# Channel sums on VectorE, weights' low parts by adding DMAs, and block-diagonal values with the mean as a bias, in a two-block sequence model on one core

## The chip, the cores and the metric

One core of a Trainium2 chip runs the whole program: two layers of a first block and one layer of a second block, on 512 positions of 1024 channels. The metric is device time in microseconds.

## The reference

All arithmetic is float32. A layer of the first block mixes by two branches, then adds a cross-attention and a gated feed-forward part; the second block follows. The change touches the mixing part only:

```python
def mlstm_branch(xm, z, ...):
    xc = silu(causal_dwconv(xm, conv_w, conv_b))
    q, k, v = blockdiag(xc, wq), blockdiag(xc, wk), blockdiag(xm, wv)   # blocks of 4x4
    gates = concatenate([q, k, v]) @ w_gate + b_gate
    h = mlstm_chunkwise(heads(q), heads(k), heads(v), i_pre, f_pre)     # 4 heads of 256
    hn = (h - mean(h)) * rsqrt(var(h) + 1e-5)
    return ((hn * norm_g + skip * xc) * silu(z)) @ w_down

def conformer_conv_branch(a, g, ...):
    u = causal_dwconv(a * sigmoid(g), dw_w, dw_b)                       # 31 taps
    u = silu(layernorm(u, ln_g, ln_b))                                  # mean and variance over 1024 channels
    return u @ w_pw + b_pw
```

## The kernel before

Channels lie on partitions (8 tiles of 128), the 512 positions on columns. Every float32 product is made of three in a faster format: `wsplit` loads a weight block of 128x1024 (512 KB) into `r`, ACT rounds it into a high part `h`, and VectorE takes `l = r - h`. `dense` runs 8 x 3 matmuls of 128x512 per output tile: high weights by high and low operand, low weights by high operand. The buffers of `h` and `l` turn over in threes (`wh`), those of `r` in twos. All loads are issued from SyncE's queue (line 183); GpSimd (POOL) has no DMA.

`mix` is the part in question, once per layer. It projects the conformer's gate and value (16 dense products), then multiplies small block-diagonal weights with each other (float32 matmuls of 36 and 128 columns), then runs the 8 mLSTM projections with their convolution of 4 taps, then the gates, then 4 heads. 16 more dense products, the output gates, are set among the gates' chain and the heads as fillers (`fill`). Then come 8 products for `z` with the mLSTM's output `ym`, then the products by `ml_w_down`, then those by `cv_w_pw`.

The conformer's convolution of 31 taps (`conv31`) is background work on VectorE: 248 steps, handed out a few per dense product (`pump`) at a low priority, into 8 tiles `acc`. The layer norm over channels needs two sums over all 1024 channels. Before, `totals` multiplies each of the 8 tiles by a matrix of ones in plain float32 and lets PSUM add them; first the tiles, then their squares once the mean is subtracted.

The values of a head come from `xm` by block-diagonal weights from which the mean over the head is taken: ACT adds a bias to the weights, which makes 256 columns per half head full, so each position block needs two float32 matmuls of 256 columns added together.

The order on each engine is made at build time by a scheduler that plays the program on a timeline; rows of that order stand with the change below. Names in the trace are cut: `h` and `l` are the weights' parts, `r` the raw block, `p` a PSUM tile, `t` and `w` other tiles.

Of the kernel before, what the change touches and what calls it, by code (L numbers as in the profile page):

```python
# [20 lines left out]
P = 128  # L21
# [8 lines left out]
# columns of the parameter arrays (per layer: mixers, the rest; second block): name -> (first column, columns)  # L30
# [29 lines left out]
def consts():  # L60
    """Identity; where a chunk's key is in reach; 2^100 where the time lies behind."""
    s, t = np.arange(P)[:, None], np.arange(P)[None, :]
    c = np.stack([s == t, (s <= t) & (s // 64 == t // 64), s > t]).astype(np.float32)
    c[2] = np.where(s > t, np.float32(2.0**100), np.float32(0))
    return c


def consts2():
    """Row selectors [36, 4, 128] (rows h and 32 + h) and the scan's resets."""
    c = np.zeros((2, P, T), np.float32)  # L70
    for h in range(4):
        c[0, [h, 32 + h], P * h : P * h + P] = 1.0
    c[1] = (np.arange(T) % 64 != 0).astype(np.float32)[None, :]
    return c
# [13 lines left out]

class Net:
    def __init__(self, tc, D, es):  # L90
# [11 lines left out]
        self.bg, self.rate, self.debt = [], 0.0, 0.0  # L102
        self.ahead = []
# [81 lines left out]
    def pump(self):  # L185
        """Some of the background work."""
# [14 lines left out]
    def split_into(self, h, l, src, scale=None):  # L201
        """The two parts of src * scale, a high one of 12 bits and the rest."""
# [17 lines left out]
    def wsplit(self, src, k, n):  # L220
        """A weight block [128, k, n] from DRAM and its two parts."""
# [4 lines left out]
        self.split_into(h, l, r)  # L226
        return h, l

    def dense(self, W, m, ops, n=T, mw=P):
        """PSUM [mw, n] = W[:, tile m]^T @ ops (list of (hi, lo) per 128 channels)."""  # L230
# [12 lines left out]
    def rsqrt(self, v, eps, y):  # L243
        """y = -2 / sqrt(v + eps); v in PSUM or SBUF."""
# [22 lines left out]
    def totals(self, xs, which):  # L267
        """total of several tiles"""
        ps = self.psum(tag="pf")
        for j, x in enumerate(xs):  # L270
            self.mm(ps, self.ones[:, which], x, j == 0, j == len(xs) - 1)
        return ps

    def square(self, x):
        q = self.w()
        self.act(q, x, AF.Square)
        return q

    def parts(self, xs, g, tag="hn"):
        """The parts of x * g (g a column per tile)."""  # L280
        return [self.split(x, g[:, j : j + 1], tag=tag) for j, x in enumerate(xs)]

    def norm(self, xs, g, tag="hn"):
        """rms norm; g holds the gain times -1/2. The parts of x * g, and what their products are to be times."""
# [44 lines left out]
    def silu2(self, pre):  # L329
        """2 * silu(pre), in place."""  # L330
# [16 lines left out]
    def gate(self, d, W, m, j, ops, bias=0.0):  # L347
        """tanh of half a gate, kept in DRAM."""
# [5 lines left out]
    def gated(self, d, j, ps):  # L354
        """(1 + the kept tanh) * ps"""
# [4 lines left out]
    def rows_bcast(self, src):  # L360
        """[4, T] float32 as the parts of one operand [36, T]; read with self.sel."""
# [6 lines left out]
    def conv31(self, u, acc):  # L368
        """Background steps: depthwise conv of u (twice its value)."""
        for j in range(KT):  # L370
# [8 lines left out]

            self.bg.append(first)  # L380
            for k in range(29, -1, -1):
                self.bg.append(lambda k=k, j=j: tap(k, j))

    def mix(self, l, xs, xd):
# [4 lines left out]
        u, acc = [], []  # L389
# [20 lines left out]
        # products of the weights: gates from xc and xm, scores from xc alone  # L410
# [26 lines left out]
        # the values' weights less their means over the heads  # L437
# [4 lines left out]
        wv = []  # L442
        for h in range(4):
            b = self.t((P, 2, 256))
            self.dma(b, D["wv"][l][:, 2 * h : 2 * h + 2])
            for c in range(2):
                self.act(b[:, c], b[:, c], AF.Identity, bias=r[:, 2 * h + c : 2 * h + c + 1])
            wv.append(b)
        # mLSTM: conv and gate (xc twice its value)
        xm, xc = [], []  # L450
        xcd = self.dp.tile([KT, P, T], F32, name=self.nm("xcd"))
        for j in range(KT):
            if j == BV:
# [3 lines left out]
                self.act(ev, pe, AF.Copy)  # L457
            pm = self.dense(win, j, hn)
# [21 lines left out]
        # gates  # L480
# [4 lines left out]
        bi, bf = self.pc("gate_b", 0)[:4], self.pc("gate_b", 1)[32:36]  # L485
        W4 = (4, T)
        f, i_, B = self.t(W4), self.t(W4), self.t(W4)
        self.act(f, pg[32:36], AF.Identity, bias=bf)
        self.act(i_, pg[0:4], AF.Identity, bias=bi)
# [17 lines left out]
        pu = self.psum((P, 4, 4), tag="pf")  # L507
        for j in range(4):
            nc.tensor.transpose(pu[:, j], i_[:, P * j : P * j + P], self.ident[:4, :4])
        uT = self.small((P, 4, 4), 2, "uT")  # L510
# [4 lines left out]
        for h in range(4):  # L515
# [14 lines left out]
            for k0 in (0, 2):  # L530
                pv = self.psum((P, 2, 256))
                for k in (k0, k0 + 1):
                    for c in range(2):
                        self.mm(pv[:, k - k0], xm[2 * h + c][:, P * k : P * k + P], wv[h][:, c], c == 0, c == 1)
                a, b = self.split(pv, shape=(P, 2, 256))
# [41 lines left out]
        fill(16)  # L577
        y, vv = self.w(W4), self.w(W4)
# [28 lines left out]
        # conformer branch: layer norm, swish  # L607
        pmu = self.totals(acc, 0)
        mg = []
        for j in range(KT):  # L610
# [4 lines left out]
            if j == 1:  # L615
                for k in range(KT):
                    self.tt(acc[k], acc[k], pmu, ALU.subtract)
                r = self.rsqrt(self.totals([self.square(c) for c in acc], 0), 1, self.t(tag="R"))
# [32 lines left out]
    def memory(self):  # L651
        """The parts of the normalised memory."""
# [137 lines left out]
    def between(self, xs):  # L790
        """The first block's norm and at once the second block's first one."""
# [34 lines left out]
    def finish(self, w2, a, xs, out):  # L826
        """The last tile of the sum, the norm and the stores, one half of the times after the other."""
# [20 lines left out]
    def cmul(self, ore, oim, are, aim, bre, bim, tmp, neg=False):  # L848
        """(are + i aim)(bre + i bim); with neg, the negated imaginary part."""
# [582 lines left out]
```

## Time and profile before

| | us |
|---|---|
| median of 3 runs (lowest, highest) | 3160.26 (3159.73, 3161.98) |
| profiled execution, span | 3160.4 |
| TensorE busy | 3120.6 (99%) |
| weight loads busy (beside matmuls) | 2548.6 (81%) |
| VectorE busy | 2098.6 (66%) |
| ScalarE busy | 1351.1 (43%) |
| GpSimd busy | 0.7 (0%) |
| DMA, mean share of 16 engines | 35.2% |

The span runs from the first to the last instruction of the profiled execution, which is one more run; it stands as that execution's own time. A busy time counts time in which at least one instruction of the engine ran. A float32 matmul shows as two records, one in the faster format as one.

### The profile page before, as it was taken

The page shows a single profiled execution, that of the slowest core. Times are in us where ns is not written, and L with a number is a line of the kernel's source. Part 1 is how long each engine was busy: PE and PEld are TensorE (multiplying, and loading weights), DVE is VectorE, ACT ScalarE, POOL GpSimd, SP SyncE. Part 2 cuts the span into 40 slices and gives each one's busy share as a digit, 9 for nine tenths or more (in the row PEclk, how much of TensorE's full clock was granted, in tenths as well). Part 3 has the DMA queues.
Part 4 walks back from the last instruction along what each step waited for, and adds up shares of the span by engine and source line. Part 5 has one row for each costly group of instructions (what it writes and reads, how often), then busy time and mean ns, then how long its engine had stood idle before and what let it go on. Part 6 is the DMA issues. An engine that isn't in the chain of part 4 may idle for free. (4 is left out here: it accounts for less than half of the span.)

```text
span 3160.4 us, 37385 instructions
## 1 busy us (share of the span) xinstructions
PE 3120.6 (99%) x14508; PEld 2548.6 (81%) x14508; DVE 2098.6 (66%) x3191; ACT 1351.1 (43%) x1923; POOL 0.7 (0%) x5
## 2 busy tenths in 40 slices
PE   8989999999999999999999999999999999999998
PEld 7867778888888887777888888888888788788887
DVE  8988975558773798886556876365534873655533
ACT  6444454446552444445444555332223433442222
POOL 0000000000000000000000000000000000000000
PEclk9999999999999999999999999999999999999999
DMA  5322443323333433245332333332333354532332
GB/s 174 118 89 80 163 148 122 114 80 100 96 103 114 121 117 106 76 161 161 112 107 87 100 97 94 96 100 95 99 102 116 107 142 120 190 100 94 100 94 87
DMA packets 135041, 354.29 MB, mean 112 GB/s; under 512 B 23472, under 2 KB 31936, under 8 KB 134864
## 3 DMA queue, kind: packets, MB, share of 16 engines
q1 hardware_dynamic: 134864, 351.92, 35.2%
q8 instruction: 113, 1.85, 0.2%
q14 instruction: 64, 0.52, 0.1%
HBM read 318.60 MB, written 29.85 MB: 110 GB/s over the span
## 5 line engine op out<-in xcount | busy, mean ns | idle before, releaser
L180 PE MATMUL p<-t,h 128*128 128x512 f32 (+1 forms) x8092 | 2470.7, 387 | 12.8 <-ACT h L167 10.7
L180 PEld LDWEIGHTS p<-t,h 128*128 128x128 f32 x8092 | 1507.0, 188 | 335.5 <-issue 16.5
L180 PE MATMUL p<-t,l 128*128 128x512 f32 (+1 forms) x4046 | 1561.4, 387 | 3.6 <-DVE l L170 2.6
L167 ACT ACTIVATE h<-r 128x1024 fp32r<-128x1024 f32 (+2 forms) x541 | 556.7, 1030 | 1301.6 <-PE p L180 826.5
L170 DVE TENSOR_TENSOR l<-r,h 128x1024 fp32r<-128x1024 f32 (+2 forms) x541 | 640.4, 1185 | 435.4 <-ACT h L167 434.3
L180 PEld LDWEIGHTS p<-t,l 128*128 128x128 f32 x4046 | 761.3, 188 | 164.3 <-DVE l L170 5.7
L177 DVE SCALAR_TENSOR_TENSOR t<-t,mph,t 128x489 f32<-128x489 f32 (+19 forms) x480 | 341.4, 729 | 6.8 <-ACT t L167 2.3
L180 PE MATMUL p<-t,t 128*128 128x256 f32 (+9 forms) x1528 | 258.5, 319 | 2.8 <-DVE t L170 2.0
L170 DVE TENSOR_TENSOR w<-p,t 128x512 f32<-128x512 f32 (+1 forms) x204 | 124.0, 622 | 191.7 <-PE p L180 189.4
L180 PEld LDWEIGHTS p<-t,t 128*128 128x128 f32 (+5 forms) x1528 | 199.1, 178 | 51.4 <-issue 18.3
L167 ACT ACTIVATE t<-w 128x512 fp32r<-128x512 f32 (+2 forms) x204 | 121.2, 598 | 165.6 <-DVE w L170 100.4
L170 DVE TENSOR_TENSOR t<-p,t 128x512 fp32r<-128x512 f32 (+2 forms) x156 | 96.9, 632 | 125.1 <-PE p L180 94.8
L177 DVE SCALAR_TENSOR_TENSOR t<-w,t 128x512 fp32r<-128x512 f32 (+1 forms) x208 | 141.9, 685 | 16.8 <-ACT t L167 14.8
L177 DVE SCALAR_TENSOR_TENSOR w<-w,fp,w 128x511 f32<-128x511 f32 (+1 forms) x176 | 131.8, 749 | 13.4 <-ACT w L167 10.3
L167 ACT ACTIVATE w<-w,fp 128x512 f32<-128x512 f32 x176 | 134.5, 764 | 8.7 <-DVE w L170 5.6
L167 ACT ACTIVATE w<-t 128x512 f32<-128x512 f32 (+2 forms) x160 | 95.1, 609 | 31.1 <-DVE t L177 15.4
L170 DVE TENSOR_TENSOR w<-w,w 128x512 f32<-128x512 f32 (+2 forms) x153 | 102.3, 674 | 8.3 <-ACT w L167 6.6
L167 ACT ACTIVATE w<-w 128x512 f32<-128x512 f32 (+2 forms) x110 | 68.0, 620 | 69.9 <-DVE w L177 66.5
L177 DVE SCALAR_TENSOR_TENSOR w<-w,w 128x512 f32<-128x512 f32 (+2 forms) x115 | 78.2, 681 | 27.9 <-ACT w L167 27.8
L167 ACT ACTIVATE t<-p 128x512 fp32r<-128x512 f32 (+3 forms) x118 | 61.8, 537 | 73.2 <-PE p L180 56.2
L170 DVE TENSOR_TENSOR w<-p,w 128x512 f32<-128x512 f32 x45 | 31.0, 691 | 74.2 <-PE p L180 74.2
L180 PE MATMUL p<-h,t 128*128 128x256 f32 (+1 forms) x320 | 68.5, 306 | 0.0
(147 smaller groups left out, 1213.6 us busy)
## 6 DMA issues: line engine op xcount, KB each, us to landing
r<-ffn_w SPq DMA_DIRECT2D x120, 512.0 KB, 3.4
r<-w_in SPq DMA_DIRECT2D x96, 512.0 KB, 3.5
r<-ffn_w_up SPq DMA_DIRECT2D x88, 512.0 KB, 3.5
r<-ffn_w_down SPq DMA_DIRECT2D x32, 512.0 KB, 3.6
r<-w_out SPq DMA_DIRECT2D x24, 512.0 KB, 3.6
tg<-g SPq DMA_DIRECT2D x32, 256.0 KB, 2.0
r<-ml_w_down SPq DMA_DIRECT2D x16, 512.0 KB, 3.5
w<-tg SPq DMA_DIRECT2D x32, 256.0 KB, 4.4
```

The costliest lines, as they stand in the source:

```text
L167: self.nc.scalar.activation(out, in_, f, **k)
L170: self.nc.vector.tensor_tensor(out=out, in0=a, in1=b, op=op)
L177: self.nc.vector.scalar_tensor_tensor(out=out, in0=a, scalar=s, in1=b, op0=op0, op1=op1)
L180: self.nc.tensor.matmul(ps, lhsT=l, rhs=r, start=start, stop=stop)
```

## The change

Three edits, all in `mix` and what it calls:

- Sums: `conv31` also adds the finished tiles into one tile on VectorE, as background; the squares are added on VectorE by `sumsq`. One matmul by ones each (`total`) replaces eight.
- Low parts: from before the mLSTM projections to the last head (`lean`), `wsplit` writes `-h` into `l` by a second ACT copy, and a DMA from GpSimd's queue adds the weights from DRAM to it. That holds for 8 projections and 16 output gates per layer.
- Values: the weights stay block-diagonal (two matmuls of 128 columns in place of two added ones of 256). The negated mean of the weights goes as four more columns into the gates' product, comes out as four more rows, is transposed with the gates, and is added to the values as a bias when these are split.

```diff
+class Tiles(list):
+    sum = None
...
         self.dma(r, src)
-        self.split_into(h, l, r)
+        if not self.lean:
+            self.split_into(h, l, r)
+            return h, l
+        self.act(h, r, AF.Copy)
+        self.act(l, r, AF.Copy, scale=-1.0)
+        self.nc.gpsimd.dma_start(out=l, in_=src, accum_op=ALU.add)
         return h, l
...
-    def totals(self, xs, which):
-        ps = self.psum(tag="pf")
-        for j, x in enumerate(xs):
-            self.mm(ps, self.ones[:, which], x, j == 0, j == len(xs) - 1)
-        return ps
...
+            def add(j=j):
+                if j == 1:
+                    acc.sum = self.t(tag="R")
+                if j:
+                    self.tt(acc.sum, acc[0] if j == 1 else acc.sum, acc[j], ALU.add)
...
-        for h in range(4):
-            b = self.t((P, 2, 256))
-            self.dma(b, D["wv"][l][:, 2 * h : 2 * h + 2])
-            for c in range(2):
-                self.act(b[:, c], b[:, c], AF.Identity, bias=r[:, 2 * h + c : 2 * h + c + 1])
-            wv.append(b)
+        wv = blocks("wv")
+        self.lean = True
...
+                for h in range(4):
+                    nc.vector.tensor_copy(out=ev[:, 2 * h : 2 * h + 2, 4 + h], in_=r[:, 2 * h : 2 * h + 2])
...
-            nc.tensor.transpose(pu[:, j], i_[:, P * j : P * j + P], self.ident[:4, :4])
+            nc.tensor.transpose(pu[:, j], i8[:, P * j : P * j + P], self.ident[:8, :8])
...
-                        self.mm(pv[:, k - k0], xm[2 * h + c][:, P * k : P * k + P], wv[h][:, c], c == 0, c == 1)
-                a, b = self.split(pv, shape=(P, 2, 256))
+                        self.mm(pv[:, k - k0, P * c : P * c + P], xm[2 * h + c][:, P * k : P * k + P], wv[2 * h + c])
+                a, b = (self.t((P, 2, 256), F32R) for _ in range(2))
+                for k in range(2):
+                    mean = uT[:, k0 + k, 4 + h : 5 + h]
+                    self.act(a[:, k], pv[:, k], AF.Identity, bias=mean)
+                    self.stt(b[:, k], pv[:, k], mean, a[:, k].bitcast(F32), ALU.add, ALU.subtract)
...
         fill(16)
+        self.lean = False
...
-        pmu = self.totals(acc, 0)
+        pmu = self.total(acc.sum, 0)
...
-                r = self.rsqrt(self.totals([self.square(c) for c in acc], 0), 1, self.t(tag="R"))
+                r = self.rsqrt(self.total(self.sumsq(acc), 0), 1, self.t(tag="R"))
```

The order of the instructions moves with it. First place: TensorE in layer 0, from the last product of the gates (p_1487) to the transposes (by `identr`) and the broadcasts (by `sel`). p_1712, p_1630, p_1673 and p_1716 are dense products of the output gates. Before:

```order
L180 MATMUL p_1487<-t_1481,t_995 36x512
L180 MATMUL p_1487<-t_1471,t_993 36x512
L180 MATMUL p_1712<-t_319,h_1714 128x512
...
L180 MATMUL p_1712<-t_355,l_1715 128x512
L180 MATMUL p_1764<-t_1092,t_1003 128x512
...
L180 MATMUL p_1772<-t_1146,t_1004 128x512
L509 MATMUL p_1755<-identr,t_1521 128x4 x4
L180 MATMUL p_1780<-t_1539,sel 128x512
```

and with the change:

```order
L187 MATMUL p_1487<-t_1481,t_995 36x512
L187 MATMUL p_1487<-t_1471,t_993 36x512
L187 MATMUL p_1630<-t_331,l_1633 128x512
...
L187 MATMUL p_1630<-t_355,l_1633 128x512
L187 MATMUL p_1673<-t_313,h_1675 128x512
...
L187 MATMUL p_1716<-t_355,l_1719 128x512
L514 MATMUL p_1759<-identr,t_1521 128x8 x4
L187 MATMUL p_1776<-t_1136,t_1004 128x512
L187 MATMUL p_1786<-t_1539,sel 128x512
```

Between the last gate product and the transposes stood 27 matmuls; now 66 do.

Second place: VectorE at the end of the conformer's convolution in layer 0. The tap of 128x482 is the last; p_3132 and p_3172 hold the mean; l_ is a low part of the next weights. Before:

```order
L177 SCALAR_TENSOR_TENSOR t_3143<-w_3141,p_3144 128x512
L177 SCALAR_TENSOR_TENSOR t_1744<-t_918,mph_91,t_1744 128x482
L177 SCALAR_TENSOR_TENSOR t_3178<-w_3176,p_3179 128x512
L170 TENSOR_TENSOR l_3363<-r_3361,h_3362 128x1024
L170 TENSOR_TENSOR l_3398<-r_3396,h_3397 128x1024
L170 TENSOR_TENSOR t_461<-t_461,p_3132 128x512
```

and with the change:

```order
L184 SCALAR_TENSOR_TENSOR t_1853<-t_918,mph_91,t_1853 128x482
...
L177 TENSOR_TENSOR t_734<-t_734,t_1853 128x512
...
L177 TENSOR_TENSOR t_461<-t_461,p_3172 128x512
...
L177 TENSOR_TENSOR t_1853<-t_1853,p_3172 128x512
L177 TENSOR_TENSOR w_3254<-w_3252,w_3254 128x512
L184 SCALAR_TENSOR_TENSOR t_3176<-w_3174,p_3177 128x512
L184 SCALAR_TENSOR_TENSOR t_3211<-w_3209,p_3212 128x512
L177 TENSOR_TENSOR l_3396<-r_3394,h_3395 128x1024
L177 TENSOR_TENSOR l_3431<-r_3429,h_3430 128x1024
```

The two low parts stood ahead of the eight subtractions of the mean and now stand behind them.

Third place: ACT in the mLSTM projections of layer 0. Before:

```order
L167 ACTIVATE h_1588<-r_1587 128x1024
L167 ACTIVATE t_1417<-p_1378,mp_90 128x512
L167 ACTIVATE t_1200<-t_1192 128x512
L167 ACTIVATE t_1419<-t_1417,mp_90 128x512
L167 ACTIVATE w_1261<-t_1256 128x512
L167 ACTIVATE h_1630<-r_1629 128x1024
```

and with the change:

```order
L174 ACTIVATE h_1588<-r_1587 128x1024
L174 ACTIVATE t_1416<-p_1376,mp_90 128x512
L174 ACTIVATE l_1589<-r_1587 128x1024
L174 ACTIVATE t_1418<-t_1416,mp_90 128x512
L174 ACTIVATE t_1260<-t_1252 128x512
L174 ACTIVATE w_1312<-t_1307 128x512
L174 ACTIVATE h_1632<-r_1631 128x1024
```

The second copy of the block stands behind the evacuation of a projection.

## Rows read from the trace of the kernel before

**Rows 1.** The page's first part: span, and busy time of TensorE.

```profile
span 3160.4 us, 37385 instructions
PE 3120.6 (99%) x14508; PEld 2548.6 (81%) x14508; DVE 2098.6 (66%) x3191; ACT 1351.1 (43%) x1923; POOL 0.7 (0%) x5
```

**Rows 2.** Waits of TensorE: who, for whom, us in total, times, longest.

```profile
PE p L180 <- DVE t L170: 8.0, 4, 4.9
PE p L509 <- DVE t L170: 3.8, 1, 3.8
```

**Rows 3.** Stretches: length, then busy time by engine, granted clock, DMA share, GB/s.

```profile
104.00:160.00 56.00, 56.00 (x252) 44.94 (x252) 54.53 (x82) 29.31 (x45) 0.00 (x0) 0.97 0.39 132
160.00:330.00 170.00, 161.32 (x732) 122.40 (x731) 145.69 (x217) 73.12 (x130) 0.00 (x0) 0.97 0.27 89
```

**Rows 4.** Timeline of TensorE, channel sums: start, us, instruction, count.

```profile
383.97 6.17 PE L180 MATMUL p<-t,ones 128*128 128x512 f32 x14
...
1408.83 7.03 PE L180 MATMUL p<-t,ones 128*128 128x512 f32 x16
```

**Rows 5.** The page's groups: additions of 128x512 on VectorE.

```profile
L170 DVE TENSOR_TENSOR w<-w,w 128x512 f32<-128x512 f32 (+2 forms) x153 | 102.3, 674 | 8.3 <-ACT w L167 6.6
```

**Rows 6.** Timeline of TensorE, values of a head in layers 0 and 1.

```profile
264.74 1.89 PE L180 MATMUL p<-t,t 128*128 128x256 f32 x8
...
1232.62 3.62 PE L180 MATMUL p<-t,t 128*128 128x256 f32 x16
```

**Rows 7.** Timeline of TensorE, float32 matmuls of few columns in layer 1.

```profile
1137.21 5.52 PE L180 MATMUL p<-t,t 128*128 128x36 f32 x48
...
1158.91 1.87 PE L180 MATMUL p<-t,t 128*128 128x36 f32 x16
```

**Rows 8.** Timeline of TensorE, the gates of layer 0; idle before in brackets.

```profile
188.37 1.61 PE L180 MATMUL p<-t,t 128*36 128x512 f32 x4
...
194.79 1.52 PE L180 MATMUL p<-t,t 128*128 128x512 f32 x6
200.08 0.55 PE L509 MATMUL p<-identr,t 4*128 4x4 f32 x4 [3.76 <-DVE t L170]
205.55 1.22 PE L180 MATMUL p<-t,sel 36*128 36x512 f32 x2 [4.92 <-DVE t L170]
...
211.75 0.81 PE L180 MATMUL p<-t,h 128*128 128x512 f32 x2
```

**Rows 9.** Stretches around that hole, columns as in rows 3.

```profile
206.00:208.00 2.00, 2.00 (x5) 1.16 (x5) 1.97 (x4) 1.05 (x3) 0.00 (x0) 0.50 0.00 0
...
210.00:212.00 2.00, 2.00 (x11) 1.77 (x10) 1.93 (x4) 0.60 (x1) 0.00 (x0) 1.00 0.00 0
```

**Rows 10.** Timelines of ACT and VectorE in the mLSTM projections of layer 0.

```profile
141.91 1.06 ACT L167 ACTIVATE h<-r 128x1024 fp32r<-128x1024 f32 x1 [1.91 <-PE p L180]
...
147.35 1.06 ACT L167 ACTIVATE h<-r 128x1024 fp32r<-128x1024 f32 x1 [2.95 <-PE p L180]
148.32 0.67 ACT L167 ACTIVATE t<-p,mp 128x512 f32<-128x512 f32 x1
...
149.25 1.22 DVE L170 TENSOR_TENSOR l<-r,h 128x1024 fp32r<-128x1024 f32 x1
```

**Rows 11.** DMA: the queue; then issues with count, KB each, median us to landing.

```profile
q1 hardware_dynamic: 134864, 351.92, 35.2%
...
r<-w_in SPq DMA_DIRECT2D x96, 512.0 KB, 3.5
...
t<-wkT SPq DMA_DIRECT2D x4, 256.0 KB, 6.6
```

**Rows 12.** Timelines of TensorE and VectorE at the channel mean of layer 0.

```profile
399.74 1.13 PE L180 MATMUL p<-t,ones 128*128 128x512 f32 x2 [0.51 <-DVE t L177]
...
402.61 0.50 PE L180 MATMUL p<-t,l 128*128 128x512 f32 x1 [1.28 <-DVE l L170]
...
402.47 4.86 DVE L170 TENSOR_TENSOR t<-t,p 128x512 f32<-128x512 f32 x8
```

More of the change, by code (lines that the diff above doesn't have):

```diff
@@ L265, in total @@
         return ps
-    def totals(self, xs, which):
-        ps = self.psum(tag="pf")
-        for j, x in enumerate(xs):
-            self.mm(ps, self.ones[:, which], x, j == 0, j == len(xs) - 1)
-        return ps
[L274 to L277, printed above, removed]
     def parts(self, xs, g, tag="hn"):
@@ L382, in conv31 @@
                 self.bg.append(lambda k=k, j=j: tap(k, j))
+            self.bg.append(add)
     def mix(self, l, xs, xd):
@@ L388, in mix @@
         raw, R = self.norm(xs, g, "hd")
-        u, acc = [], []
+        u, acc = [], Tiles()
         for j in range(KT):
@@ L441, in mix @@
         self.ts(r, r, -1.0 / 256, ALU.mult)
-        wv = []
-        for h in range(4):
-            b = self.t((P, 2, 256))
-            self.dma(b, D["wv"][l][:, 2 * h : 2 * h + 2])
-            for c in range(2):
-                self.act(b[:, c], b[:, c], AF.Identity, bias=r[:, 2 * h + c : 2 * h + c + 1])
-            wv.append(b)
+        wv = blocks("wv")
+        self.lean = True
         xm, xc = [], []
@@ L484, in mix @@
             self.mm(pg, ev[:, j], xm[j], False, j == KT - 1)
-        bi, bf = self.pc("gate_b", 0)[:4], self.pc("gate_b", 1)[32:36]
+        bi, bf = self.pc("gate_b", 0)[:8], self.pc("gate_b", 1)[32:36]
         W4 = (4, T)
-        f, i_, B = self.t(W4), self.t(W4), self.t(W4)
+        f, i8, B = self.t(W4), self.t((8, T)), self.t(W4)
+        i_ = i8[0:4]
         self.act(f, pg[32:36], AF.Identity, bias=bf)
-        self.act(i_, pg[0:4], AF.Identity, bias=bi)
+        self.act(i8, pg[0:8], AF.Identity, bias=bi)
         e = self.w(W4)
@@ L506, in mix @@
         fill(FILLS[0])
-        pu = self.psum((P, 4, 4), tag="pf")
+        pu = self.psum((P, 4, 8), tag="pf")
         for j in range(4):
-            nc.tensor.transpose(pu[:, j], i_[:, P * j : P * j + P], self.ident[:4, :4])
-        uT = self.small((P, 4, 4), 2, "uT")
+            nc.tensor.transpose(pu[:, j], i8[:, P * j : P * j + P], self.ident[:8, :8])
+        uT = self.small((P, 4, 8), 2, "uT")
         self.act(uT, pu, AF.Copy)
@@ L577, in mix @@
         fill(16)
+        self.lean = False
         y, vv = self.w(W4), self.w(W4)
@@ L1380, in layout @@
         o[n] = both(lambda l: blockdiag(A[s][l]).transpose(2, 1, 0))
-    b = np.zeros((DEPTH, P, 4, 2, 2, P), np.float32)
-    v = both(lambda l: blockdiag(A["ml_wv"][l])).reshape(DEPTH, P, 4, 2, P)
-    for c in range(2):
-        b[:, :, :, c, c] = v[:, :, :, c]
-    o["wv"] = b.reshape(DEPTH, P, KT, 256)
+    o["wv"] = both(lambda l: blockdiag(A["ml_wv"][l]))
     o["wvn"] = A["ml_wv"].reshape(DEPTH, KT, P, 4).transpose(0, 2, 1, 3)
```

## The prediction

> **What bounds the kernel now.** I read the page's first part, then TensorE's waits, then a table of stretches. TensorE is busy 3120.6 of 3160.4 us [rows 1], so about 40 us of the span are not its work, and nearly every matmul taken out shortens the kernel. The waits show the largest of those 40 us: one of 3.76 us before a transpose (L509) and one of 4.92 us behind VectorE [rows 2]. Both lie in layer 0, near 200 us. The stretches show why: in the first layer's mLSTM projections (104 to 160 us) VectorE is busy 54.53 of 56.00 us, and TensorE all of them; in the gates and heads (160 to 330 us) TensorE loses 8.7 us while VectorE works 145.69 of 170 us [rows 3]. VectorE is the second bound, in that part only. Layer 1 runs the same code without such waits. The profiled execution (span 3160.4 us) lies 0.1 us from the median of the three runs, 3160.26, so the sum is made against 3160.4.
>
> **A. Channel sums.** The change removes 14 float32 matmuls of 128x512 per layer (two totals of eight become two of one), 28 in all. A float32 matmul has two records. Sixteen of them in a row take 7.03 us and fourteen 6.17 us [rows 4], so two records, one matmul, are 0.86 us. 28 x 0.86 = **24.1 us** off TensorE. In return VectorE gets 14 additions of 128x512 per layer at 0.67 us [rows 5], 9.4 us. Seven run as background among the convolution taps, and the subtractions taken off VectorE (D) more than pay for those. The seven that add the squares stand on the path, see E.
>
> **B. Values.** Per layer 32 float32 matmuls lose half their columns (256 to 128). Sixteen records of the long form take 3.62 us and eight 1.89 us: 1.73 us for four matmuls, 0.43 us each [rows 6]. For the short form, a row of 48 records takes 5.52 us; by the code 32 of them have 36 columns, the other 16 have 128. Sixteen of 36 columns alone take 1.87 us, 0.117 each, so the 16 of 128 columns take 5.52 - 32 x 0.117 = 1.78 us, 0.22 us per matmul [rows 7]. 64 x (0.43 - 0.22) = **13.4 us**. The bias makes two ACT and two VectorE instructions out of one each, and eight activations on weights go; both engines have idle time there [rows 3], so nothing on the path.
>
> **C. The hole in layer 0.** The chain of gates (sigmoid, two scans, the broadcast of the maximum) keeps the transposes waiting until 200.08 and the broadcasts until 205.55; TensorE had run dry at 196.3 [rows 8]. Its granted clock fell to 0.50 after it went idle, that is from the 2.4 to the 1.2 GHz level, and was back by 210 [rows 9]; the work from 205.55 to 211.75 would take 0.23 x 3 + 8 x 0.43 = 4.1 us at the level before, so 2 us more are lost. The hole is 3.76 + 4.92 + 2.0 = 10.7 us. The order of TensorE shows what fills it: before, 27 matmuls stand between the last gate product and the transposes, now 66. At 5.44 us per 24 [rows 10] that is 6.1 us of cover before and 15.0 us now, against a chain of about 15.6 us from the last gate product (190.0) to the broadcasts. I take **10 us**.
>
> **D. Adding DMAs.** For 24 weight blocks per layer, 48 in all, VectorE's subtraction (1.22 us) becomes an ACT copy as long as the first (1.06 us) [rows 10] and a DMA from POOL's queue that adds 512 KB. POOL had no work in this part, so nothing queues behind it there. ACT gets 25 us per layer and has 27 of 56 and 97 of 170 us free [rows 3]. VectorE loses 29 us per layer. TensorE must not wait for a low part. Dense products follow one another every 5.44 us; three buffers turn over. From a released buffer: 1.06 + 0.67 (the evacuation that now stands between) + 1.06 = 2.8 us on ACT, the DMA, then 5.0 us from the first use of the low part to the product's end. Three buffers carry that without loss while (2.8 + D + 5.0)/3 is at most 5.44, so D up to **8.5 us** is free. No row shows an adding DMA. Bounds: a plain load of the block lands in 3.5 us; the slowest loads in a crowd land 256 KB in 6.6 us [rows 11], so twice that, 13.2 us, is the other end. I take twice the plain load, 7 us, since it reads two operands where a load reads one and its row is the nearest: **0 us**. At the lower end nothing is gained either, as TensorE doesn't wait on low parts there now. At 13.2 us each product takes 7.0 instead of 5.44; 8 projections and about 5 gates per layer stand back to back, so 26 x 1.56 = 41 us are lost.
> The Trainium skill (Collectives: The Full Stack, "The bandwidth ceiling") has the DMA engines add at half the rate of a copy because two sources are read; no run here shows it.
>
> **E. New waits.** Taking work from TensorE takes cover away. Layer 0: the order of VectorE now has the last tap, the last sum, and then all eight subtractions of the mean before the low parts of the next weights; before, those low parts stood first and TensorE waited 0.51 + 1.28 us [rows 12]. Eight subtractions take 4.86 us [rows 12]. From the mean's matmul I count 1.9 us to the first three, 0.6 for the last low part of the mLSTM output, 3.1 for five more, 1.8 for three short operations and 2.3 for two low parts: 10 us, in which TensorE has about 4.5 us of work. That is 5 us idle; 3 more where the eight-fold sum used to fill time while VectorE finished the outputs. Layer 1: between the mean and the total of squares stand 33 matmuls (7.5 us), while the chain between them is 4.9 us of subtractions, 7 x 0.67 of additions, and 4 us of other VectorE work between them: 13.6 us, so 6 us idle. Less the 1.8 us that go, 12 us; with 2 us for a fallen clock as in C, **+14 us**. Bounds: 0 (VectorE, with 29 us less to do, runs ahead) and 24.1 (all of A given back).
>
> **Sum:** 24.1 + 13.4 + 10 - 14 = 33.5 us, so 3160.4 - 33.5 = **3127 us**.
>
> **Rivals.**
> 1. *No new waits.* E is nothing: 3160.4 - 47.5 = 3113 us. For it: layer 1 has no wait on VectorE now. Against: the order of VectorE puts long work ahead of what TensorE needs. Chance 0.20.
> 2. *VectorE's chain takes back the sums.* E is all of A (24.1 us: 3137 us), up to A and B together (37.5 us: 3150 us). For it: VectorE is the last to finish in layer 0 [rows 12]. Chance 0.12.
> 3. *The DMA engines become the bound; slower.* A load's work per engine: 0.352 x 16 x 3160.4 us for 351.92 MB [rows 11] is 1.66 us per 512 KB. With an adding DMA of k loads, a product costs (1 + k) x 1.66 us of every engine. Up to k = 2.3 this stays under 5.44. It eats the whole gain when a product takes 33.5/26 = 1.29 us more, at k = 3.1 (5.1 us per adding DMA); at k = 4 it takes 8.3 us, 26 x 2.86 = 74 us, so 3201 us. For it: the share of the DMA engines is already 0.39 in that stretch [rows 3]. Against: two reads and a write are not four loads. Chance 0.13.
> 4. *POOL can't issue beside VectorE; slower.* VectorE works without a gap for tens of us in this stretch. If an issue must wait for one, and 10 us come on top of the 7, D is 17 us, a product takes 8.3 us, and the time is again 3201 us. No row has POOL at work beside VectorE. The Trainium skill (SBUF — State Buffer, the "DVE blocks DMA" trap) states that such a DMA's descriptors are written by GpSimd, which VectorE can lock out of a shared port; its section "Who interferes with whom" narrows that for two-input instructions, which nearly all here are, to GpSimd work that reads SBUF. By that rule this is unlikely. Chance 0.05.
>
> That the change doesn't do what it says is no rival: the order shows the removed matmuls gone and 48 adding DMAs on POOL's queue.
>
> **How the numbers follow.** My forecast has 0.50, the rivals 0.20, 0.12, 0.13 and 0.05. A measurement tells about 0.2% from no change, 6.3 us. The forecast, rival 1 and rival 2 are faster by more, but for 0.02 of slack on the last: 0.80. That and the mild end of rival 3 (0.03) fall within: 0.05. Slower is the rest of rivals 3 and 4: 0.15. The range runs from 3108 us (rival 1 and 5 us of waits elsewhere that a freer VectorE removes) to 3172 us (D at its upper bound, 3127 + 41, and a little); it leaves out the worst of rivals 3 and 4 and little below.
>
> **What would show it.** Right: TensorE's busy time down by some 38 us; no wait near 200 us in layer 0 and no fall of the clock there; waits of about 5 us on VectorE in each layer around the total of the squares; low parts landing within 8.5 us. Wrong: TensorE waiting for a DMA of low parts during the projections, a DMA share near 1 there, or products more than 5.44 us apart.

## The result, and the profile after

The changed kernel took 3128.71 us (median of 4 runs, 3125.27 to 3130.98); the kernel before, on the same chip, 3159.99 (4 runs, 3156.57 to 3161.98). The ratio is **0.9899, 95% interval 0.9886 to 0.9912**: about 32 us faster. The forecast was 3127.0 us, range 3108 to 3172. The profiled execution of the changed kernel took 3125.27 us with a span of 3123.5, so it lies 3.4 us below its median.

The page of the changed kernel: span, busy times, the DMA queues (packets, MB, share of 16 engines), and the loads and adding DMAs of weights (`w_in` holds those of the projections; KB each, median us to landing).

```profile
span 3123.5 us, 37404 instructions
...
PE 3085.6 (99%) x14452; PEld 2528.4 (81%) x14452; DVE 2068.9 (66%) x3195; ACT 1391.9 (45%) x1971; POOL 42.2 (1%) x53
...
q1 hardware_dynamic: 134288, 350.87, 36.4%
q0 software_dynamic: 6912, 25.17, 4.3%
...
r<-w_in SPq DMA_DIRECT2D x96, 512.0 KB, 4.0
...
l<-w_in POOLq DMA_DIRECT2D x48, 512.0 KB, 6.9
...
r<-ml_w_down SPq DMA_DIRECT2D x16, 512.0 KB, 3.6
```

TensorE is busy 35.0 us less than in [rows 1]. A second queue is there, and an adding DMA lands in 6.9 us.

Stretches of the changed kernel, columns as in [rows 3].

```profile
104.00:160.00 56.00, 56.00 (x249) 42.41 (x248) 55.14 (x93) 36.75 (x51) 6.91 (x8) 1.00 0.88 209
160.00:330.00 170.00, 170.00 (x808) 130.89 (x808) 145.92 (x229) 95.10 (x161) 11.22 (x13) 1.00 0.57 147
...
360.00:380.00 20.00, 15.79 (x66) 11.76 (x64) 18.38 (x33) 10.54 (x17) 0.00 (x0) 1.00 0.25 87
380.00:400.00 20.00, 17.66 (x65) 14.04 (x66) 13.71 (x19) 9.52 (x12) 0.00 (x0) 0.83 0.31 107
1340.00:1400.00 60.00, 54.62 (x221) 41.56 (x220) 48.15 (x71) 28.21 (x41) 0.00 (x0) 0.97 0.45 156
1380.00:1400.00 20.00, 14.62 (x50) 9.66 (x49) 16.83 (x25) 10.25 (x14) 0.00 (x0) 0.91 0.17 53
```

From 160 to 330 us TensorE works without a gap; before it lost 8.7 us there [rows 3]. The DMA share in the projections rose from 0.39 to 0.88, and TensorE lost nothing by it. The idle time sits elsewhere now: 4.2 and 2.3 us from 360 to 400 in layer 0, and 5.4 us from 1380 to 1400 in layer 1, with the granted clock at 0.83 and 0.91 as means of the stretches. Those two places are where each layer takes the channel mean and the total of squares.

TensorE's timeline in the changed kernel: the transposes and broadcasts of the gates, then the two places.

```profile
193.56 0.41 PE L514 MATMUL p<-identr,t 8*128 8x8 f32 x4
...
194.33 0.49 PE L187 MATMUL p<-t,sel 36*128 36x512 f32 x1
...
371.69 1.02 PE L187 MATMUL p<-t,ones 128*128 128x512 f32 x2
...
375.29 0.50 PE L187 MATMUL p<-t,h 128*128 128x512 f32 x1 [1.89 <-DVE t L184]
...
378.39 0.73 PE L187 MATMUL p<-t,h 128*128 128x512 f32 x2 [1.45 <-ACT h L174]
382.35 0.80 PE L187 MATMUL p<-t,l 128*128 128x512 f32 x1 [3.22 <-DVE l L177]
382.94 1.05 PE L187 MATMUL p<-t,h 128*128 128x512 f32 x2
...
387.96 0.61 PE L187 MATMUL p<-t,h 128*128 128x512 f32 x2
...
1388.69 0.96 PE L187 MATMUL p<-t,h 128*128 128x512 f32 x3 [2.47 <-ACT t L174]
...
1392.62 0.74 PE L187 MATMUL p<-t,h 128*128 128x512 f32 x2 [0.93 <-ACT h L174]
1394.96 2.08 PE L187 MATMUL p<-w,ones 128*128 128x512 f32 x2 [1.61 <-DVE w L177]
```

The hole of 3.76 and 4.92 us at the gates [rows 8] is gone: transposes and broadcasts have no idle time before them. In layer 0 three waits, 6.6 us in all, follow the mean; in layer 1 four, 5.4 us. VectorE's timeline in layer 0 shows what stands ahead of the operands that TensorE waits for.

```profile
368.97 0.72 DVE L184 SCALAR_TENSOR_TENSOR t<-t,mph,t 128x482 f32<-128x482 f32 x1
...
372.75 1.88 DVE L177 TENSOR_TENSOR t<-t,p 128x512 f32<-128x512 f32 x3 [1.18 <-PE p L187]
374.55 0.68 DVE L184 SCALAR_TENSOR_TENSOR t<-w,t 128x512 fp32r<-128x512 f32 x1
375.15 3.07 DVE L177 TENSOR_TENSOR t<-t,p 128x512 f32<-128x512 f32 x5
378.13 0.69 DVE L177 TENSOR_TENSOR w<-w,w 128x512 f32<-128x512 f32 x1
...
379.93 2.36 DVE L177 TENSOR_TENSOR l<-r,h 128x1024 fp32r<-128x1024 f32 x2
```

The sum by ones is one matmul now, 1.02 us at 371.69, where fourteen records took 6.17 [rows 4] and two more 1.13 [rows 12]. VectorE: last tap at 368.97, three subtractions of the mean, the last low part of the mLSTM's output (374.55, TensorE's wait of 1.89), five subtractions, the first addition of squares; only behind them two low parts of weights (379.93), for which TensorE waits 3.22 us. On ACT, squares stand ahead of the high parts of the next weights as well (three from 373.53, one at 376.78). But the first of these high parts, at 375.82, waits 0.47 us for TensorE, so the squares are not the whole of the wait of 1.45 us.

In layer 1 TensorE waits for no low part of weights. VectorE has done the eight subtractions by 1386.8; only then comes the product that ends the mLSTM's last output, and ACT's copy of it, for which TensorE waits 2.47 us:

```profile
1387.28 0.69 DVE L177 TENSOR_TENSOR w<-w,t 128x512 f32<-128x512 f32 x1
...
1388.01 0.63 ACT L174 ACTIVATE t<-w 128x512 fp32r<-128x512 f32 x1
```

### The profile page after: what moved, and what is told of

Same layout as the page of the kernel before. It is cut to its first block, busy times and chain, and to the rows that moved or that the text cites. A ratio compares the mean times of both kernels' runs of the same rounds, so it can differ in the third digit from the quotient of the medians.

```text
span 3123.5 us, 37404 instructions
## 1 busy us (share of the span) xinstructions
PE 3085.6 (99%) x14452; PEld 2528.4 (81%) x14452; DVE 2068.9 (66%) x3195; ACT 1391.9 (45%) x1971; POOL 42.2 (1%) x53
## 3 DMA queue, kind: packets, MB, share of 16 engines
q1 hardware_dynamic: 134288, 350.87, 36.4%
## 5 line engine op out<-in xcount | busy, mean ns | idle before, releaser
L187 PE MATMUL p<-t,h 128*128 128x512 f32 (+1 forms) x8092 | 2470.9, 387 | 17.9 <-ACT h L174 11.5
L177 DVE TENSOR_TENSOR l<-r,h 128x1024 fp32r<-128x1024 f32 (+3 forms) x493 | 582.8, 1184 | 423.4 <-ACT h L174 422.6
L187 PE MATMUL p<-t,t 128*128 128x256 f32 (+9 forms) x1528 | 243.5, 308 | 2.8 <-DVE t L177 2.0
L187 PEld LDWEIGHTS p<-t,t 128*128 128x128 f32 (+5 forms) x1528 | 187.7, 176 | 44.9 <-issue 14.8
L177 DVE TENSOR_TENSOR t<-p,t 128x512 fp32r<-128x512 f32 (+2 forms) x140 | 86.1, 627 | 120.1 <-PE p L187 93.0
L184 DVE SCALAR_TENSOR_TENSOR w<-w,fp,w 128x511 f32<-128x511 f32 (+1 forms) x176 | 132.0, 750 | 13.3 <-ACT w L174 10.2
L177 DVE TENSOR_TENSOR w<-w,w 128x512 f32<-128x512 f32 (+2 forms) x167 | 112.3, 678 | 8.1 <-ACT w L174 5.9
L184 DVE SCALAR_TENSOR_TENSOR w<-w,w 128x512 f32<-128x512 f32 (+2 forms) x115 | 78.3, 682 | 26.6 <-ACT w L174 26.4
L174 ACT ACTIVATE t<-p 128x512 fp32r<-128x512 f32 (+3 forms) x102 | 51.8, 520 | 65.5 <-PE p L187 48.7
```

What stands on the lines that cost most here:

```text
L174: self.nc.scalar.activation(out, in_, f, **k)
L177: self.nc.vector.tensor_tensor(out=out, in0=a, in1=b, op=op)
L184: self.nc.vector.scalar_tensor_tensor(out=out, in0=a, scalar=s, in1=b, op0=op0, op1=op1)
L187: self.nc.tensor.matmul(ps, lhsT=l, rhs=r, start=start, stop=stop)
```

## Experiments

To compare traces I use one more measure: each trace was cut into stretches of 10 us, and in each stretch TensorE's busy time times (1 - granted clock) was summed as **clock loss**; busy time less clock loss is **work**, what TensorE would take at full clock. Idle time and clock loss "in the layers" are those from 60 to 600 and from 1100 to 1600 us. The kernel before has 3106.4 us of work, and 11.0 us of idle time and 4.3 of clock loss in the layers; the changed one 3071.3, 14.0 and 3.9. Differences in us below are from the ratio to the kernel before on the same chip, times 3160.3.

### One part undone

**Sums back on TensorE.** `totals` and `square` are as before, and `conv31` adds nothing:

```diff
-            self.bg.append(add)
...
-        pmu = self.total(acc.sum, 0)
+        pmu = self.totals(acc, 0)
...
-                r = self.rsqrt(self.total(self.sumsq(acc), 0), 1, self.t(tag="R"))
+                r = self.rsqrt(self.totals([self.square(c) for c in acc], 0), 1, self.t(tag="R"))
```

> The changed kernel with both channel sums back on TensorE (28 float32 matmuls). My theory (sums worth 24.1 us of TensorE and costing about 14 us of new waits around the total of squares): the time rises by 24 - 14 = 10 us against the changed kernel, to about 3139 us; TensorE busy rises by 24, the idle time at 360 to 400 us and 1380 to 1400 us (now 6.6 and 5.4 us) goes; the gates' hole near 200 us stays closed. Rival (the idle time there comes from the freer order, not from the sums: VectorE is late with its convolution anyway): the idle time stays, and the time rises by the full 24 us, to 3153 us.

Measured: 3136.4 us, ratio 0.9926 (0.9913 to 0.9938), 8.5 us slower than the changed kernel. Work 3093.7, that is 22.4 us more; idle time in the layers 1.0 us in place of 14.0. So the new waits belong to the sums, and the gates' hole stays closed without them. The theory holds, the rival falls.

**No adding DMAs.**

```diff
-        self.lean = True
```

> The changed kernel without the adding DMAs: VectorE subtracts the low parts everywhere. The scheduler's order has 26 matmuls between the last gate product and the transposes here, as before the change (27), not 66. My theory (the low parts cost and gain nothing by themselves, but the order that they bring closes the gates' hole): the hole of about 10 us near 200 us with its clock fall is back, TensorE busy is as in the changed kernel within 3 us, time about 3139 us, or a few us more where VectorE, with 29 us per layer more to do, is later at the channel sums. Rival 1 (the hole is closed by the values' edit): it stays closed, 3129 us. Rival 2 (the adding DMAs cost something, since DMA engines are 0.88 busy in the projections): faster than 3127 us.

Measured: 3168.83 us, ratio 1.0030 (1.0018 to 1.0042): **slower than the kernel before**, and 41 us slower than the changed kernel. Neither the theory (3139) nor a rival came near. TensorE's timeline of this kernel:

```profile
197.29 0.38 PE L513 MATMUL p<-identr,t 8*128 8x8 f32 x4 [2.85 <-ACT t L174]
203.91 1.22 PE L187 MATMUL p<-t,sel 36*128 36x512 f32 x2 [6.24 <-DVE t L177]
...
420.08 2.08 PE L187 MATMUL p<-w,ones 128*128 128x512 f32 x2 [8.00 <-DVE w L177]
```

The hole at the gates is back, as forecast. What was not forecast is the rest: 40.7 us of idle time and 15.4 of clock loss in the layers. Of the idle time 9.1 us lie at the gates of layer 0 (8.7 before), 5.1 in the heads of layer 1, and 26.6 around the end of the convolution (380 to 450 and 1410 to 1470 us). VectorE's timeline of layer 0 says why.

```profile
396.97 6.80 DVE L184 SCALAR_TENSOR_TENSOR t<-t,mph,t 128x490 f32<-128x490 f32 x9
```

The last nine taps run from 396.97 to 403.8; in the changed kernel the last tap began at 368.97. Against the kernel before TensorE has shed 32 us of work, but VectorE ends the convolution no sooner, 34 us later than in the changed kernel.

**Values as before.** Weights of 256 columns with the mean taken off by ACT, two added matmuls:

```diff
-                        self.mm(pv[:, k - k0, P * c : P * c + P], xm[2 * h + c][:, P * k : P * k + P], wv[2 * h + c])
+                        self.mm(pv[:, k - k0], xm[2 * h + c][:, P * k : P * k + P], wv[h][:, c], c == 0, c == 1)
```

> The changed kernel with the values of before (float32 matmuls of 256 columns, two added). My theory: TensorE busy rises by 13.4 us and the time with it, to about 3142 us, all else the same. Rival (values were partly hidden, or their evacuation in two pieces costs ACT and VectorE more than it saves): the time rises by less than 8 us.

Measured: 3140.19 us, ratio 0.9938 (0.9926 to 0.9951), 12.3 us slower than the changed kernel; work 16.6 us more. As expected.

### One part alone

Edits as above, the other two parts undone. The three kernels complete the table of all eight combinations.

> The kernel before with the sums' edit alone. No_lean showed that sums and values without the adding DMAs are slower than before (1.003), by 27 us more idle time of TensorE than the two take off its work. Theory 1 (the steps add: 24.1 us off, 14 us of new waits): 3150 us. Theory 2 (without the adding DMAs VectorE is late by its whole backlog at the sums, and takes back what TensorE saves): 3156 to 3163 us, with 20 us or more of idle time around the total of squares, the gates' hole as before.

> The kernel before with the adding DMAs alone. 68 matmuls between the last gate product and the transposes (27 before). Theory 1 (they gain the gates' hole and nothing else): 10.7 us, 3149.5 us, TensorE busy as before. Theory 2 (they are worth the 40 us that no_lean lost): 3120 us; this can't be the whole, as TensorE is busy 3120.6 us before and has some 30 us of idle time, of which 10 lie at start and end; so by theory 2 most of the 40 us appears only where sums and values are edited too.

> The kernel before with the values' edit alone. Theory 1 (the steps add): 13.4 us off, 3147 us. Theory 2 (VectorE is the bound of the stretch from projections to heads, so what TensorE saves there comes back as waits): 3155 to 3163 us, idle time of TensorE up by 5 us or more in the gates and heads of both layers.

| parts in | ratio to before (95%) | us against before | work | idle and clock loss in the layers |
|---|---|---|---|---|
| none | 1 | 0 | 3106.4 | 11.0 + 4.3 |
| sums | 1.0024 (1.0015 to 1.0034) | +7.6 | 3086.9 | 30.1 + 13.4 |
| values | 1.0033 (1.0020 to 1.0046) | +10.4 | 3095.9 | 26.0 + 10.2 |
| sums, values | 1.0030 (1.0018 to 1.0042) | +9.5 | 3074.3 | 40.7 + 15.4 |
| adding DMAs | 0.9957 (0.9942 to 0.9972) | -13.6 | 3107.7 | 1.7 + 1.7 |
| adding DMAs, sums | 0.9938 (0.9926 to 0.9951) | -19.6 | 3087.9 | 11.5 + 5.2 |
| adding DMAs, values | 0.9926 (0.9913 to 0.9938) | -23.4 | 3093.7 | 1.0 + 1.7 |
| all three | 0.9899 (0.9886 to 0.9912) | -31.9 | 3071.3 | 14.0 + 3.9 |

Theory 2 holds in kind in all three, not in size. Both kernels without adding DMAs came out slower than it said (3167.99 and 3173.05 us, not at most 3163). With the values alone the idle time grew behind the convolution and not in the gates, where it is 8.4 us against 8.7. With the adding DMAs alone the 13.6 us are also within noise of theory 1's 10.7; it is the table as a whole that shows where the other 28 us lie. Sums alone and values alone take 19.5 and 10.5 us off TensorE's work and make the kernel **slower**; alone the three changes would add up to +4.4 us, together they give -31.9. The last column is the answer: without the adding DMAs, every microsecond that TensorE saves comes back as idle time and lost clock, and more. With them, sums and values are worth 6.0 and 9.8 us each (the 6.0 not clear of noise: the intervals overlap), and with the other in as well they are worth 8.5 and 12.3.

VectorE's timeline of the kernel before shows the last tap of layer 0,

```profile
398.97 0.72 DVE L177 SCALAR_TENSOR_TENSOR t<-t,mph,t 128x482 f32<-128x482 f32 x1
```

that of the kernel with the values alone its last two,

```profile
403.08 1.47 DVE L184 SCALAR_TENSOR_TENSOR t<-t,mph,t 128x483 f32<-128x483 f32 x2
```

that of the kernel with the sums alone,

```profile
399.97 1.48 DVE L184 SCALAR_TENSOR_TENSOR t<-t,mph,t 128x483 f32<-128x483 f32 x2
```

and that of the kernel with the adding DMAs alone the last.

```profile
355.70 0.72 DVE L184 SCALAR_TENSOR_TENSOR t<-t,mph,t 128x482 f32<-128x482 f32 x1
```

With VectorE subtracting the low parts, the convolution of layer 0 ends between 399 and 405 us (in the kernel before the matmul by ones that waits for it starts at 399.74 [rows 12]), however little TensorE has to do; with the adding DMAs alone 43 us earlier. VectorE sets the end of that part of the layer. In layer 1 it is not even as early as before: the last tap of the kernel before,

```profile
1403.16 0.71 DVE L177 SCALAR_TENSOR_TENSOR t<-t,mph,t 128x482 f32<-128x482 f32 x1
```

comes 22 us later with the sums alone,

```profile
1425.01 0.72 DVE L184 SCALAR_TENSOR_TENSOR t<-t,mph,t 128x482 f32<-128x482 f32 x1
```

and ends 24 to 26 us later with the values or with both; in the four kernels with adding DMAs it ends between 1331 and 1338. Why a part alone costs more than it saves is settled in part only: the clock loss is in the table, the sums also give VectorE 14 additions per layer, and with the values alone the last tap ends 5 us later than before (404.6 against 399.7). Each of these kernels has an order of its own from the scheduler. How much is VectorE's load and how much the order was not separated.

### How much the adding DMAs can bear

**Each adding DMA twice.**

```diff
-        self.act(l, r, AF.Copy, scale=-1.0)
-        self.nc.gpsimd.dma_start(out=l, in_=src, accum_op=ALU.add)
+        self.act(l, r, AF.Copy, scale=-2.0)
+        for _ in range(2):
+            self.nc.gpsimd.dma_start(out=l, in_=src, accum_op=ALU.add)
```

> The changed kernel with every adding DMA issued twice, onto twice the negative (so the low parts of these 24 weight blocks per layer count twice: the output differs a little). In the changed kernel an adding DMA landed in 6.9 us and took 4.3% of 16 engines for 25.17 MB, 2.8 us per engine and block, 1.65 loads of 1.70 us; the DMA engines are 0.88 busy from 104 to 160 us. Twice makes a product cost 1.70 + 5.6 = 7.3 us of every DMA engine against 5.44 us of TensorE. Theory (the change stands close under the DMA bound, free up to a landing of 8.5 us): products 7.3 us apart where they stand back to back, 26 of them, 48 us slower than the changed kernel, about 3177 us, and TensorE waits for the DMA of low parts. Rival (there is slack: buffers and fillers take up the delay): within 10 us of the changed kernel.

Measured: 3193.12 us, ratio 1.0102 (1.0085 to 1.0119), 64 us slower than the changed kernel. TensorE's waits for these DMAs:

```profile
PE p L187 <- DMA l<-w_in: 41.7, 19, 4.0
```

POOL's timeline in the projections (start, us, two issues each; in brackets POOL's wait before them),

```profile
118.46 1.76 POOL L239 DMA_DIRECT2D l<-w_in  x2 [6.94 <-DMA l<-w_in]
126.80 1.76 POOL L239 DMA_DIRECT2D l<-w_in  x2 [6.58 <-DMA l<-w_in]
135.14 1.76 POOL L239 DMA_DIRECT2D l<-w_in  x2 [6.58 <-DMA l<-w_in]
```

and a stretch, columns as before.

```profile
104.00:160.00 56.00, 47.02 (x186) 35.94 (x186) 38.85 (x66) 22.94 (x31) 10.54 (x12) 0.88 0.91 205
```

Products are 8.34 us apart here, not 7.3: POOL issues the second addition of one block and the first of the next (1.76 us), then waits 6.58 us for that one to land before it can issue the second onto it. Two issues and one landing set the pace, and the DMA engines, 0.91 busy, are little fuller than in the changed kernel (0.88). By 26 products that is 26 x (8.34 - 5.44) = 75 us against 64 measured. TensorE does wait for these DMAs, as the theory had it, but for another reason than full engines, and 16 us more than it said; so this run doesn't show how close the change stands to a bound of the DMA engines.

**Adding DMAs through z and `ml_w_down`.** `self.lean = False` moves from behind the heads to behind the products by `ml_w_down`.

> The changed kernel with the adding DMAs kept on through the products for z and by ml_w_down: 16 more per layer, so VectorE loses another 20 us per layer, just ahead of and in the stretch with the new waits, and ACT gains 17 us. Theory (VectorE's backlog is what the adding DMAs relieve: they were worth 40 us in the changed kernel, 13.7 us alone): the low parts no longer wait behind the subtractions, idle time in the layers falls by 6 us or more, 3114 to 3122 us. Rival 1 (there the low part must follow a chain of ACT copy, issue and landing of 1.06 + 0.9 + 6.9 us, and ACT's queue holds the eight squares ahead of it): TensorE waits for ACT or the DMA instead, time the same or slower, 3127 to 3140 us. Rival 2 (DMA engines): waits on the low parts' DMA as in the run with two adding DMAs (41.7 us there).

Measured: 3139.79 us, ratio 0.9934 (0.9921 to 0.9946), 11 us **slower** than the changed kernel. Rivals 1 and 2 hold. TensorE's waits,

```profile
PE p L187 <- DMA l<-ml_w_down: 14.4, 5, 4.6
```

the DMA issues (KB each, median us to landing),

```profile
r<-ml_w_down SPq DMA_DIRECT2D x16, 512.0 KB, 7.7
l<-ml_w_down POOLq DMA_DIRECT2D x16, 512.0 KB, 8.4
```

and a stretch, columns as before.

```profile
1340.00:1400.00 60.00, 57.00 (x236) 44.45 (x234) 36.33 (x59) 33.90 (x49) 6.90 (x8) 0.97 0.91 246
```

In that stretch the DMA engines are 0.91 busy (0.45 in the changed kernel). The plain load of `ml_w_down` lands in 7.7 us where it took 3.6, and only then can ACT write what the DMA adds to, for another 8.4. VectorE is busy 36 of 60 us there, 48 in the changed kernel: it was not full there, so there was less to relieve.

### The new waits around the channel sums

**Later.** The block behind `if j == 1:` moves to `j == 3`.

> The changed kernel with the subtraction of the mean, the sum of squares and what follows written two products by ml_w_down later (behind the fourth in place of the second), so the low parts of two more products stand ahead of it for the scheduler; 50 and 70 matmuls stand between mean and total of squares, where 44 and 33 stood. My theory (the new waits are a matter of VectorE's order and the cover): the idle time around the total of squares falls from about 12 us to 4 or less and the time by 6 to 12 us, to about 3119 us. Rival (the chain's length behind the last tap of the convolution sets it): the wait moves to the products by cv_w_pw, and the time stays within 3 us of the changed kernel.

Measured: 3126.80 us, ratio 0.9897 (0.9883 to 0.9911): no difference that can be told. Idle time in the layers fell from 14.0 to 11.4 us only; in layer 0 the eight subtractions still stand ahead of the low parts, since the scheduler takes what is ready, and the subtractions are ready first. My theory failed; the time stayed within the rival's 3 us, but the waits did not move on as the rival had it: one new wait of 0.9 us stands behind them, at 415.68.

**Squares ahead.** The variance is computed as the mean of the squares less the square of the mean.

```diff
+            if c >= 0:
+                self.squares(acc, acc.n - 1)
         self.drain()
...
-        pmu = self.total(acc.sum, 0)
+        self.squares(acc, KT)
...
+        pmu, psq = self.total(acc.sum, 0), self.total(acc.sq, 0)
+        mu, r, m2 = acc.sum, acc.sq, self.w()
+        self.act(mu, pmu, AF.Copy)
+        self.act(m2, pmu, AF.Square)
+        self.tt(m2, psq, m2, ALU.subtract)
+        self.rsqrt(m2, 1, r)
...
-                for k in range(KT):
-                    self.tt(acc[k], acc[k], pmu, ALU.subtract)
-                r = self.rsqrt(self.total(self.sumsq(acc), 0), 1, self.t(tag="R"))
...
+                    self.tt(c, c, mu, ALU.subtract)
```

> The changed kernel with the variance as mean of squares less square of the mean: the squares are taken and added while the output z is projected, a tile behind the convolution, so that between the two totals no subtraction, square or addition is left. The work is the same but for two short operations. Theory (the new waits, 14.0 us idle and 3.9 us of fallen clock in the two layers, come from the chain from the mean to the total of squares, which holds low parts and operands of the next products back on VectorE and ACT): idle time and clock loss fall to 6 us or less, 3113 to 3121 us. Rival (moving that chain by two products gained nothing in later3, so the waits come from VectorE's backlog ahead of the mean, the last taps and outputs): idle time stays above 10 us, the time within 4 us of the changed kernel's 3128.7.

Measured: 3121.99 us, ratio 0.9886 (0.9870 to 0.9901), 4 us better by the ratios, with intervals that overlap. Idle time and clock loss in the layers are 11.7 + 2.9 in place of 14.0 + 3.9, where the theory asked for 6 or less: it failed, and the squares were the smaller part. The profiled execution is 4.7 us shorter than the changed kernel's, but 3.8 us of that are clock loss outside the layers (6.6 in place of 10.4 us), where the edit changes nothing; so a gain in time is not shown. TensorE's largest wait in the layers,

```profile
383.32 0.79 PE L188 MATMUL p<-t,l 128*128 128x512 f32 x1 [2.97 <-DVE l L178]
```

is still for a low part behind the block of subtractions on VectorE:

```profile
377.23 4.90 DVE L178 TENSOR_TENSOR t<-t,t 128x512 f32<-128x512 f32 x8 [0.65 <-ACT t L175]
382.05 1.22 DVE L178 TENSOR_TENSOR l<-r,h 128x1024 fp32r<-128x1024 f32 x1
```

**Both together**, squares ahead and the longer use of adding DMAs:

> Both together: squares ahead, and adding DMAs through z and ml_w_down. If chain and backlog are two separate causes, the gains add (idle time in the layers near 2 us, 3108 to 3114 us); if they are the same wait seen from two sides, it is no better than the better of the two alone; if the adding DMAs wait for ACT, it is slower than the squares alone.

Measured: 3142.20 us, ratio 0.9938 (0.9925 to 0.9950), as slow as the longer use alone: there TensorE waits 13.2 us for the adding DMAs of `ml_w_down`, as without the squares ahead (14.4).

**Mean late.** On top of squares ahead, the mean comes off only after the product with the inverse deviation, so that nothing is ready before the deviation is.

```diff
+        self.tt(mu, mu, r, ALU.mult)
...
-                    self.tt(c, c, mu, ALU.subtract)
                     self.stt(c, c, self.pn("cv_ln_g")[:, k : k + 1], r, ALU.mult, ALU.mult)
+                    self.stt(c, mu, self.pc("cv_ln_g", k, h=True), c, ALU.mult, ALU.add)
```

> Squares ahead, and the mean taken off after the product with the inverse deviation in place of before it (eight operations of two inputs in place of eight subtractions, and one product of mean and deviation more). In squares_ahead the eight subtractions still stand as one block of 4.90 us on VectorE (377.23) ahead of the next low part, and TensorE waits 2.97 us for it; in this order two low parts stand ahead of the block. Theory (what is left of the new waits is that block): the 2.97 us go, idle time in the layers falls from 11.7 to 9 us or less, 3116 to 3120 us. Rival (the low parts then come later, behind the longer block after the deviation): the wait moves there, and the time stays within 2 us of squares_ahead's 3122.0.

Measured: 3120.61 us, ratio **0.9865 (0.9849 to 0.9882)**: the lowest of all, and its interval lies just below the changed kernel's. VectorE's timeline:

```profile
379.78 1.23 DVE L178 TENSOR_TENSOR l<-r,h 128x1024 fp32r<-128x1024 f32 x1 [2.08 <-ACT h L175]
...
381.52 1.22 DVE L178 TENSOR_TENSOR l<-r,h 128x1024 fp32r<-128x1024 f32 x1
...
386.48 4.06 DVE L185 SCALAR_TENSOR_TENSOR t<-t,mpn,t 128x512 f32<-128x512 f32 x6
```

Two low parts now stand ahead of the block. The wait of 2.97 us is gone, and idle time in the layers is 6.8 us, half of the changed kernel's (the clock loss, 5.1 us, is not lower). What the step from squares ahead to this is worth in time is not settled. The two intervals overlap, the median lies within 2 us of 3122.0, as the rival had it, and the profiled execution (3122.67 us) is longer than that of squares ahead (3120.58): what it gains in idle time it loses in clock, over half of that outside the layers. The trace shows that the wait is gone, and no more.

## Why the prediction was right, and where it was not

The time was forecast to 2 us, which is less than the noise (the interval is 4 us to either side), so that closeness is in part luck. In the traces work fell by 35.1 us and idle time and clock loss in the layers rose by 2.6, 32.5 in all against 33.5 forecast; the profiled spans differ by 36.9, as 4.9 us of idle time outside the layers, which no term had, are gone too. The sum over parts was right for the three together; what it said of each part on its own was not.

- **A, sums, 24.1 us off TensorE:** 22.4 us of work with the other parts in, 19.5 alone. **B, values, 13.4 us:** 16.6 and 10.5, on average 13.5. Together 35.1 us of work against 37.5. What one part takes off differs by up to 6 us with the others that are in, so these are rough.
- **C, the hole at the gates:** gone with its clock loss, 8.7 + 2.6 us against 10 forecast, as read from the cover of 66 matmuls. The runs add whose doing it is: idle time of 8.4 us and more from 180 to 220 us is in all four kernels without adding DMAs, and in none of the four with them. It is a gain of D.
- **D, adding DMAs, "0 us": the step that failed.** The landing was right (6.9 us against 7 taken, under the 8.5 us that are free), and TensorE waited for none. But D was priced by what it costs. VectorE's 29 us less per layer came in only as cover for A's additions, and in the bounds: no new waits, and 5 us of waits elsewhere. It is worth 13.6 us alone and 41 us with A and B in (+9.5 to -31.9). The prediction had called VectorE "the second bound"; it did not draw from it that A and B without D would gain nothing: they cost 9.5 us. Because C and the size of E were read from the order of the finished change, D's gain was in the sum all the same, under other letters.
- **E, new waits, +14 us:** 6.6 us idle in layer 0 (8 forecast), 5.4 in layer 1 (6), 3.9 us of clock loss in the layers (2). Place and order were those read from the listing, with subtractions ahead of low parts, for the largest wait of layer 0 (3.22 us). The other waits are for the last parts of the mLSTM's output, for high parts from ACT and for the sum of squares itself; in layer 1 none is for a low part of weights. That all of them come from the sums is shown by the kernel with the sums back (1.0 us idle).
- **Rival 1** (no new waits) fell. **Rival 2** (VectorE's chain takes the sums back) is what happens without D. **Rival 3** (DMA engines) fell, but was near: they are 0.88 busy, and with the longer use, at 0.91, TensorE waits for them. **Rival 4** (POOL can't issue beside VectorE) fell: VectorE is busy 55.14 of 56.00 us in the projections, and POOL's 48 issues and their landings are, in the view of the low parts' DMAs,

```profile
L238 POOL DMA_DIRECT2D l<-w_in x48: 862/862/1005, 91.5 to 1302.6; - x48
...
DMA to landing us min/median/max: 6.0/6.9/9.7
```

an issue of 0.86 us, at most 1.0, and a landing of at most 9.7. By the Trainium skill (SBUF — State Buffer, "Who interferes with whom"), a VectorE instruction with two inputs in SBUF contends with a GpSimd instruction that reads SBUF, not with one that only writes it. The trace agrees in so far as no issue was held up.

## What to carry to other kernels

When one engine is busy 99% and a second one over 90% in a stretch, price the parts of a change together: here work taken from the first gained nothing, and cost some us, until the second was relieved. Reading the order of the finished change priced the whole well, but said little on which part earns it; a table of all combinations did. Where a scheduler takes what is ready, writing a chain elsewhere moved little here; making its squares ready sooner and its subtractions later halved the layers' idle time.

## What the runs showed of the hardware

- An adding DMA of 512 KB costs each of the 16 engines 0.043 x 3123.5 / 48 = 2.8 us, a plain load 0.364 x 3123.5 x 0.524 / 350.87 = 1.70 us (shares and MB of the changed kernel's page): a factor of 1.65. The plain figure is an average over all transfers of that queue; the adding DMAs all run where the engines are fullest. The Trainium skill (Collectives: The Full Stack, "The bandwidth ceiling") has adding, in a ring between ranks, at half the rate of a copy because of its two source reads; the 1.65 measured here for a local DMA is somewhat better than that factor of 2.
- Plain loads landed later with adding DMAs beside them: the median over all loads of `w_in` went from 3.5 [rows 11] to 4.0 us, and that of `ml_w_down` from 3.6 to 7.7 where the engines were 0.91 busy.
- The waits cost more than their idle time: after those of layer 0, the last of 3.22 us, the granted clock is 0.83 as a mean from 380 to 400 us and 0.50 from 382 to 386 (the 1.2 GHz level, as in [rows 9]), and pairs of matmuls that take 0.61 us at 387.96 take 1.05 us at 382.94. Over the four kernels without adding DMAs the layers' clock loss goes with their idle time: 4.3, 10.2, 13.4, 15.4 us at 11.0, 26.0, 30.1, 40.7.
